# Conformer and S5 layer on one core: gate-row copies behind the first convolution taps, B loaded a step ahead, small matrices ahead of a tile's taps, two layer norm steps moved, last output tile halved

## Chip, core, metric

One Trainium2 chip, one of its cores, one launch. The metric is the device time of the whole kernel in microseconds (us). Data are float32; a product of two matrices is made of three TensorE passes over split operands (`hi*whi`, `lo*whi`, `hi*wlo`).

## The reference, cut to what matters

A layer with two branches beside each other over 2048 tokens of 1024 channels, with 256 tokens of context ahead of them:

```python
h = rmsnorm(x, norm_g) * (1 + scale) + shift                 # scale, shift, gate = silu(c) @ w_ada + b_ada
p = split(h @ w_in)                                          # 5 x 1024 columns: value, glu gate, conv gate, u, ssm gate
v = p[0] * sigmoid(p[1])
v = dwconv(v, 31 taps along rows or columns of a 64-wide grid) + conv_db
conv_out = silu(layernorm(v)) * silu(p[2])
y = s5(p[3]; a, b, c, both directions, state carried in from the context) + ssm_d * p[3]
y = gelu(y);  ssm_out = y * sigmoid(y @ glu_w + glu_b) * silu(p[4])
x = x + gate * (concat(conv_out, ssm_out) @ w_out)
return rmsnorm(x, final_g)
```

`gate` is a row of 1024 numbers. The S5 layer has 64 groups of 16 channels; `B` and `C` are complex matrices of a group.

## The kernel before

The kernel is one program of stages. By the trace's time: up to about 180 us the modulation and the first projections; from there to about 699 the other projections of `h`, with the convolution beside them; to about 1230 the state-space blocks; to about 1417 the GLU matrix product; to about 1791 the output product; then the end of the last output tile. The engines run their own queues in order, and a wait at the head of a queue holds everything behind it.

**Projections beside the convolution.** A projection (`project`, 24 matmuls of 512 columns, three for each of 8 slices, L129, L134 and L135) writes a bank `ps` from a pool of three. A convolution tile of 128 channels takes eight projections: four glu gates, which ScalarE evacuates (L296), and four values, which VectorE multiplies with them (`glu`, L299). So a projection can begin only when the bank of the projection three before it has been read. The 31 taps of the tile before are done on VectorE (L336, one instruction a tap and accumulator: `fP`, `fQ`, `fR`); the accumulators are begun by ScalarE (L319, L320, L323). After each projection `beside()` emits RATE = 4.8 taps, the glu products that are held, and one step of `toeplitz()`. That generator makes, for each of 16 channel groups, small matrices that the state-space stage needs, in four steps: (0) products on GpSimd; (1) every fourth group `bbar`, six VectorE products with `bq`, the loaded B, and a scratch tile `tb` (L363 to L368); (2) four VectorE additions into `ff` (L396); (3) 32 small matmuls into the bank `tz` (L407); their evacuation (`tzs`, L417 to L420) is at the head of the next group's step 0. TensorE's rows are chained in the order of the program, so a matmul of `tz` that waits holds the projections behind it.

**The gate rows.** Ahead of the first convolution tile, `gps` (one PSUM bank) collects the product of `silu(c)` with the gate columns of `w_ada` in four rows. ScalarE copies each row to a tile `gr` (L717) and SyncE stores it to `gate_d` (L718). `gr`, `tb`, `us`, and other short-lived tiles rotate through a pool `stage` with one tag, `"sa"`, of three buffers: a new tile waits until what stood in its buffer three tiles before has been used.

**Layer norm of the convolution.** It runs in four pieces of 512 tokens (`layer_norm(nb)`): load and sum (`lsum`, GpSimd), `mu` (L1069, matmul), `va` (L1082) and the reciprocal root with `dg` (L171), `rb` (L1101) with the products by it on VectorE and the silu on ScalarE, then four loads, products by the conv gate `lg` and stores to `mix_d`. The pieces are woven into TensorE's order at chosen products: piece 0 in the GLU stage by the list `aside` (`for n in (6, 10, 14, 15, 17, 18, 20, 21)`: one step after GLU product `n`), pieces 1 to 3 in the output stage by `LN_QUARTER = (0, 4, 7, 9)`.

**The output stage.** 16 tiles `t_` of 128 tokens, each with four products of 24 matmuls (half `k8` of the channels, half `i` of the columns) into `pso`. The product number within four tiles is `4 * (t_ % 4) + 2 * (1 - k8) + i`; counted over all tiles it is called product 0 to 63 here. A product needs its half of `mix_d` loaded (`mr`) and split into `mh` (ScalarE, L1026) and `ml` (VectorE, L1029), and the split rows of `w_out` (`woh`, `wol`). Tiles 4 to 7 use piece 1 of the layer norm, so product 18 (the convolution half of tile 4) is the first that needs it. The last tile ends with a square sum, a reciprocal root (`rs`), two products by `rs` and `fg` of 512 columns (L1287) and their stores (L1288).

Of the kernel before, what the change touches and what calls it, by code (L numbers as in the profile page):

```python
# [7 lines left out]
F32 = mybir.dt.float32  # L8
# [6 lines left out]
P = 128  # L15
# [10 lines left out]
GH = 16  # L26
# [6 lines left out]
LN_QUARTER = (0, 4, 7, 9)  # L33
# [44 lines left out]
def build(ctx: ExitStack, tc: tile.TileContext, ins: dict, out: bass.AP):  # L78
    nc = tc.nc
# [64 lines left out]
    for nb in (0, 1, 3):  # L144
        hpool[nb] = hstack.enter_context(tc.tile_pool(name=f"h{nb}", bufs=1, side="right"))
    nps = pstack.enter_context(tc.tile_pool(name="nps", bufs=2, space=PS))
# [154 lines left out]
    def taps(ct, v, half):  # L301
# [21 lines left out]
        act(r_, S_, AF.Identity, scale=tap[2](0), bias=db[:, 1, ct:ct + 1])  # L323
# [27 lines left out]
    def bbar(q):  # L351

        g_ = slice(16 * q, 16 * q + 16)
        shp = [P, 16, GH]
        bq = stage.tile([P, 2, 16, GH], F32, tag="sa", name="bq")
        for i, nm in enumerate(("b_re", "b_im")):
            nc.sync.dma_start(bq[:, i], ins[nm][:, g_, :])
        bb = late.fir.tile([P, 33, GH], F32, tag="bb", name="bb")
        tb = stage.tile(shp, F32, tag="sa", name="tb")
        bbr, bbn = bb[:, 0:16], bb[:, 16:32]  # L360
        nc.gpsimd.memset(bb[:, 32], 0.0)
        a, b = (t_[:, g_].unsqueeze(2).to_broadcast(shp) for t_ in (br, bi))
        dv(vt(bbr, bq[:, 0], a, op=MUL))  # L363
        dv(vt(tb, bq[:, 1], b, op=MUL))
        dv(vt(bbr, bbr, tb, op=SUB))
        dv(vt(bbn, bq[:, 0], b, op=MUL))
        dv(vt(tb, bq[:, 1], a, op=MUL))
        dv(st(bbn, bbn, -1.0, tb, op0=MUL, op1=SUB))  # L368
        return bb

    def toeplitz():

        for b4 in range(GR // 4):
            g0 = 4 * b4
            cc = late.fir.tile([P, 2, 4, GH], F32, tag="cc", bufs=2, name="cc")
            for i, nm in enumerate(("c_re", "c_im")):
                nc.sync.dma_start(cc[:, i], ins[nm][:, g0:g0 + 4, :])
            fs, sums = [], []
# [13 lines left out]
            if b4 % 4 == 0:  # L392
                bb = bbar(b4 // 4)
# [6 lines left out]
            tz = late.tps.tile([P, 2, P], F32, tag="tz", name="tz")  # L400
# [305 lines left out]
    gps = nps.tile([P, 512], F32, tag="gps", bufs=1, name="gps")  # L706
# [7 lines left out]
    for i in range(2):  # L714
        for c in range(2):
            gr = stage.tile([1, 512], F32, tag="sa", name="gr")
            act(gr, gps[64 * i + 32 * c:64 * i + 32 * c + 1], AF.Copy)  # L717
            nc.sync.dma_start(gate_d[i:i + 1, c * 512:(c + 1) * 512], gr)  # L718
# [4 lines left out]
    with tstack, tc.tile_pool(name="fir", bufs=1, reuse_waits="tile") as late.fir, \  # L723
            tc.tile_pool(name="firps", bufs=1, space=PS, reuse_waits="tile") as late.fps, \
            tc.tile_pool(name="tps", bufs=1, space=PS, reuse_waits="tile") as late.tps:
# [7 lines left out]
        def beside():  # L733

            due[0] += RATE
# [10 lines left out]
            next(toe, None)  # L746
# [37 lines left out]
        drain()  # L784
    vstack.close()
# [411 lines left out]
    for n in (6, 10, 14, 15, 17, 18, 20, 21):  # L1197
        aside[n].append(ln)
# [65 lines left out]
    with tc.tile_pool(name="op", bufs=2, reuse_waits="tile") as op:  # L1264
# [14 lines left out]
        def finish(t_, cols, xt, sq):  # L1279
# [6 lines left out]
            for cs_ in [slice(0, 1024)] if t_ < 15 else [slice(0, 512), slice(512, 1024)]:  # L1286
                st(xt[:, cs_], xt[:, cs_], rs, fg[:, cs_], op0=MUL, op1=MUL)  # L1287
                nc.sync.dma_start(ov[row(t_)[0], row(t_)[1], cs_], xt[:, cs_])  # L1288
# [3 lines left out]
        for t_ in range(16):  # L1292
# [16 lines left out]
            for k8 in (1, 0):  # L1309
# [6 lines left out]
                if t_ < 15:  # L1316
                    for i in range(2):
                        product(k8, i)
                        if k8 == 0:
                            evacuate(i, cols[i], pss[i], xt, sq)  # L1320
                        if t_ < 12 and 4 * (t_ % 4) + 2 * (1 - k8) + i in LN_QUARTER:
                            next(lns[t_ // 4 + 1])
            if t_ == 15:
                for i in range(3):
                    product(1, i)
                    product(0, i)
                    evacuate(i, cols[i], pss[i], xt, sq)
            finish(t_, cols, xt, sq)
# [75 lines left out]
```

## Time and profile before

| | |
|---|---|
| time, three runs | 1800.38, 1800.89, 1803.52 us; median 1800.89 |
| profiled execution | 1801.97 us, its span 1800.2 us |
| TensorE busy | 1725.8 us, 96% of the span |
| VectorE busy | 1410.8 us, 78% |
| ScalarE, GpSimd busy | 584.9 us (32%), 561.5 us (31%) |
| DMA engines | 39% on average |

The span is what the trace covers; the profiled execution's own time is 1.8 us longer. The share of an engine is an average over stages of very different kinds: TensorE is the busiest in all of them, but what it waits for, and which engine it is that sets its pace, must be read in each stage. A wait of TensorE costs more than its idle time, since the matmuls behind it are slower for a while.

### The profile page before, as it was taken

Reading aid. Unit: us, or ns where it says so; the run is one execution under the profiler, and the core shown is the slowest. Engines: PE = TensorE matmul, PEld = TensorE weight load, DVE = VectorE, ACT = ScalarE, POOL = GpSimd, SP = SyncE. Lnnn points to the kernel's source line nnn. Section 1 sums busy time; section 2 is a strip of 40 time slices with the busy share of each in tenths; the row PEclk is TensorE's granted clock in tenths of the full one; section 3 lists DMA queues with packets and bytes.
Section 4 is the critical chain, followed back from the end, with each engine's and each line's share of the span. In section 5 each row is a group of like instructions: output and inputs, shape, how many; then the busy total and the mean of one; then the engine's idle time right before and its main releaser. Section 6 shows DMA issues by size and latency. Waiting matters only on the chain.

```text
span 1800.2 us, 23670 instructions
## 1 busy us (share of the span) xinstructions
PE 1725.8 (96%) x8728; PEld 1354.6 (75%) x8728; DVE 1410.8 (78%) x2063; ACT 584.9 (32%) x904; POOL 561.5 (31%) x550
## 2 busy tenths in 40 slices
PE   7999799999999998999999999999989989999998
PEld 2675577787788886777777777778778768887887
DVE  7863799999998987999999999995665755656533
ACT  4542211221222113343433433354453422222211
POOL 0632243344432113665554655320210041212000
PEclk9999899999999998999999999999999999999999
DMA  9604131222222123243333333363738837363621
GB/s 342 231 18 127 34 104 44 96 79 68 97 98 76 50 76 109 88 121 106 101 117 115 98 122 105 105 225 120 215 113 279 303 108 206 118 198 122 176 97 44
DMA packets 175724, 227.45 MB, mean 126 GB/s; under 512 B 38516, under 2 KB 117492, under 8 KB 174584
## 3 DMA queue, kind: packets, MB, share of 16 engines
q1 hardware_dynamic: 175608, 225.94, 39.0%
q8 instruction: 69, 1.13, 0.3%
q14 instruction: 47, 0.39, 0.1%
HBM read 147.36 MB, written 78.52 MB: 125 GB/s over the span
## 4 chain that ended last, share of the span: by engine, by line
PE 65%; DVE 20%; DMA 6%; issue 3%; ACT 2%; POOL 2%; SPq 1%; DVEq 0%; ACTq 0%; POOLq 0%
PE ps L129 13%; PE ps L134 13%; PE ps L135 13%; PE pso L135 4%; PE pso L134 4%; PE pso L129 4%; DVE fQ L336 4%; PE S L894 3%; DVE fR L336 3%; PE Y L945 3%; DVE fP L336 3%; DMA mix_d<-lx 2%; PE Y L936 1%; DVE lo L223 1%; PE adps L620 1%
## 5 line engine op out<-in xcount | busy, mean ns | idle before, releaser
L129 PE MATMUL ps<-hi,whi 128*128 128x512 f32 x1248 | 499.1, 400 | 1.2 <-ACT v L296 1.2
L134 PE MATMUL ps<-lo,whi 128*128 128x512 f32 x1248 | 492.7, 395 | 0.0
L135 PE MATMUL ps<-hi,wlo 128*128 128x512 f32 x1248 | 491.6, 394 | 0.3 <-POOL wlo L244 0.3
L129 PEld LDWEIGHTS ps<-hi,whi 128*128 128x128 f32 x1248 | 235.9, 189 | 62.1 <-issue 9.3
L135 PEld LDWEIGHTS ps<-hi,wlo 128*128 128x128 f32 x1248 | 236.1, 189 | 55.5 <-issue 3.5
L134 PEld LDWEIGHTS ps<-lo,whi 128*128 128x128 f32 x1248 | 236.2, 189 | 53.4 <-issue 5.2
L129 PE MATMUL pso<-woh,mh 128*128 128x512 f32 (+1 forms) x528 | 206.2, 391 | 0.8 <-ACT woh L1026 0.4
L134 PE MATMUL pso<-wol,mh 128*128 128x512 f32 (+1 forms) x528 | 203.8, 386 | 2.1 <-DVE wol L1029 2.1
L135 PE MATMUL pso<-woh,ml 128*128 128x512 f32 (+1 forms) x528 | 204.4, 387 | 0.7 <-DVE ml L1029 0.5
L244 POOL TENSOR_TENSOR wlo<-wraw,whi 128x1024 fp32r<-128x1024 f32 x37 | 97.3, 2630 | 174.2 <-ACT whi L243 174.2
L336 DVE SCALAR_TENSOR_TENSOR fQ<-v,sml,fQ 128x960 f32<-128x960 f32 (+11 forms) x120 | 149.2, 1243 | 0.0
L336 DVE SCALAR_TENSOR_TENSOR fP<-v,sml,fP 128x960 f32<-128x960 f32 (+10 forms) x112 | 121.0, 1080 | 24.7 <-ACT fP L319 24.7
L336 DVE SCALAR_TENSOR_TENSOR fR<-fS,comb,fR 128x960 f32<-128x960 f32 (+11 forms) x120 | 128.1, 1067 | 0.0
L918 DVE TENSOR_TENSOR_SCAN t<-mag,t 128x287 f32<-128x287 f32 x128 | 122.0, 1011 | 0.0
L134 PEld LDWEIGHTS pso<-wol,mh 128*128 128x128 f32 x528 | 99.8, 189 | 24.7 <-DVE wol L1029 3.1
L129 PEld LDWEIGHTS pso<-woh,mh 128*128 128x128 f32 x528 | 99.8, 189 | 22.9 <-ACT woh L1026 1.4
L135 PEld LDWEIGHTS pso<-woh,ml 128*128 128x128 f32 x528 | 99.7, 189 | 21.7 <-DVE ml L1029 1.5
L243 ACT ACTIVATE whi<-wraw 128x1024 fp32r<-128x1024 f32 x37 | 39.1, 1055 | 212.2 <-PE ps L134 172.9
L129 PE MATMUL ps<-yh,gwh 128*128 128x512 f32 x256 | 100.7, 393 | 0.0
L134 PE MATMUL ps<-yl,gwh 128*128 128x512 f32 x256 | 99.9, 390 | 0.0
L135 PE MATMUL ps<-yh,gwl 128*128 128x512 f32 x256 | 99.9, 390 | 0.0
L1064 POOL TENSOR_TENSOR lsum<-lx 128x512 f32<-128x512 f32 x4 | 5.5, 1362 | 301.7 <-DMA lx<-cv_d 301.7
(295 smaller groups left out, 2804.8 us busy)
## 6 DMA issues: line engine op xcount, KB each, us to landing
wraw<-in_w_in SPq DMA_DIRECT2D x37, 512.0 KB
mr<-mix_d SPq DMA_DIRECT2D x32, 512.0 KB
wa<-in_w_ada SPq DMA_DIRECT2D x32, 256.0 KB
xt<-in_x_t SPq DMA_DIRECT2D x32, 256.0 KB
u_d<-us SPq DMA_DIRECT2D x32, 256.0 KB
f_d<-ff SPq DMA_DIRECT2D x32, 256.0 KB
cv_d<-v SPq DMA_DIRECT2D x8, 1024.0 KB
cg_d<-gs SPq DMA_DIRECT2D x32, 256.0 KB
```

Of the source, the lines that this page charges most:

```text
L129: i = nc.tensor.matmul(ps, wh, rh, start=first, stop=False)
L134: nc.tensor.matmul(ps, wh, rl, start=False, stop=False)
L135: last[0] = nc.tensor.matmul(ps, wl, rh, start=False, stop=end)
L223: st(lo, xts[k], sh_, hi.bitcast(F32), op0=ADD, op1=SUB)
L243: act(hi, raw, AF.Copy)
L244: pt(lo, raw, hi.bitcast(F32), op=SUB)
L336: yield st(at(acc, lo_ + o, hi_ + o), at(src, lo_ + j, hi_ + j), tap[n](j), at(acc, lo_ + o, hi_ + o), op0=MUL, op1=ADD)
L620: nc.tensor.matmul(adps[32 * c:32 * c + 32], sil[:, k], was[h, k, c], start=(k == 0), stop=(k == KT - 1), skip_group_check=True)
L894: m = nc.tensor.matmul(Sf[h_, o + c0:o + c1], k.E[:, d, i, h_], seq[g][d][:, c0:c1], start=True, stop=True, skip_group_check=True)
L918: nc.vector.tensor_tensor_scan(dst[:, d, 0:L], mag8[:, g0 + d:g0 + d + 1].to_broadcast([P, L]), src[:, d, 0:L], 0.0, op0=MUL, op1=ADD)
L936: m = nc.tensor.matmul(Y[:, g], k.M[:, g], k.U[:, g, NX:NCOL], start=True, stop=False, skip_group_check=True)
L945: m = nc.tensor.matmul(Y[:, g], k.F[h_, i, d], hs, start=False, stop=(i == 1 and d == 1), skip_group_check=True)
```

## The change

Five things are changed.

- The four copies of the gate rows and their stores move from ahead of the first tile's taps into the first `beside()`, behind the accumulators' begin on ScalarE (a dependency without a semaphore keeps them behind `late.fr`). `gps` and `tz` share a PSUM bank of a pool of their own, `gpp`; before, `gps` stood in the pool that was closed ahead of the convolution, and `tz` in one of its own.
- `bq` is loaded in step 0, by `b_load`, into a tile of its own in the pool `fir`; before, it was loaded in `bbar`, a step later, into the pool `stage`.
- `beside()` begins with `next(toe, None)`, ahead of its taps and glu products; before, it ended with it.
- Layer norm piece 0 has its `rb` step after GLU product 16 in place of 15, its first gate step at 18 and its second at 19. Piece 1 has its `mu`, `va` and `rb` steps one output product later: (0, 5, 8, 10).
- In the last tile each piece `xt` is multiplied by `fg` as it is evacuated (into `gx`); after `rs`, ScalarE scales columns 0 to 511 and VectorE columns 512 to 1023, and the two halves are stored from ScalarE's and SyncE's queues.

```diff
-LN_QUARTER = (0, 4, 7, 9)
+LN_QUARTER = ((), (0, 5, 8, 10), (0, 4, 7, 9), (0, 4, 7, 9))
...
+    gpp = tstack2.enter_context(tc.tile_pool(name="gpp", bufs=1, space=PS))
...
+    def b_load(q):
+        bq = late.fir.tile([P, 2, 16, GH], F32, tag="bq", name="bq")
+        for i, nm in enumerate(("b_re", "b_im")):
+            nc.sync.dma_start(bq[:, i], ins[nm][:, 16 * q:16 * q + 16, :])
+        return bq
+
+    def bbar(q, bq):
...
-        bq = stage.tile([P, 2, 16, GH], F32, tag="sa", name="bq")
-        for i, nm in enumerate(("b_re", "b_im")):
-            nc.sync.dma_start(bq[:, i], ins[nm][:, g_, :])
...
+            if b4 % 4 == 0:
+                bq = b_load(b4 // 4)
...
-            tz = late.tps.tile([P, 2, P], F32, tag="tz", name="tz")
+            tz = gpp.tile([P, 512], F32, tag="g", name="tz")[:, 0:2 * P].rearrange("p (d q) -> p d q", d=2)
...
+    def gate_out():
+        for i in range(2):
+            for c in range(2):
+                gr = stage.tile([1, 512], F32, tag="sa", name="gr")
+                g_ = act(gr, gps[64 * i + 32 * c:64 * i + 32 * c + 1], AF.Copy)
+
+                tc.add_manual_dep(g_.ins, late.fr.ins.name, mybir.DependencyInfo(
+                    mybir.DependencyClass.NoSync, mybir.DependencyReason.DATA), reason="order")
+                nc.sync.dma_start(gate_d[i:i + 1, c * 512:(c + 1) * 512], gr)
...
         def beside():
 
+            next(toe, None)
             due[0] += RATE
...
-            next(toe, None)
+            if late.fr is not None and not late.gated:
+                late.gated = True
+                gate_out()
...
-    for n in (6, 10, 14, 15, 17, 18, 20, 21):
+    for n in (6, 10, 14, 16, 18, 19, 20, 21):
...
-            for cs_ in [slice(0, 1024)] if t_ < 15 else [slice(0, 512), slice(512, 1024)]:
-                st(xt[:, cs_], xt[:, cs_], rs, fg[:, cs_], op0=MUL, op1=MUL)
-                nc.sync.dma_start(ov[row(t_)[0], row(t_)[1], cs_], xt[:, cs_])
+            if t_ < 15:
+                st(xt, xt, rs, fg, op0=MUL, op1=MUL)
+                nc.sync.dma_start(ov[row(t_)[0], row(t_)[1], :], xt)
+                return
+
+            act(xt[:, 0:512], late.gx[:, 0:512], AF.Identity, scale=rs)
+            vs(xt[:, 512:1024], late.gx[:, 512:1024], rs, None, op0=MUL)
+            nc.scalar.dma_start(ov[row(t_)[0], row(t_)[1], 0:512], xt[:, 0:512])
+            nc.sync.dma_start(ov[row(t_)[0], row(t_)[1], 512:1024], xt[:, 512:1024])
...
+                    if i == 0:
+                        late.gx = wp.tile([P, 1024], F32, tag="wraw", bufs=1, name="gx")
+                    vt(late.gx[:, cols[i]], xt[:, cols[i]], fg[:, cols[i]], op=MUL)
```

Line numbers of the changed kernel are 2 higher at the taps and the glu (L338, L301), 5 at `bbar` (L368 to L373), 7 at `ff`, `tz` and `tzs` (L403, L414, L426), 9 at the gate rows (L726) and 17 in the layer norm (L1086, L1118).

On ScalarE, at the end of the first convolution tile, the rows of before are these (`whi` and `us` belong to projections, `v` is a glu gate):

```order
L320 ACTIVATE fQ<-v,sml 128x32x32
L243 ACTIVATE whi<-wraw 128x1024
L428 ACTIVATE us<-ps 128x2x256
L296 ACTIVATE v<-ps 128x512 x2
L717 ACTIVATE gr<-gps 1x512 x4
L319 ACTIVATE fP<-v,db,sml 128x1024
L323 ACTIVATE fR<-fS,db,comb 128x1024
```

And these are the rows of the changed kernel at the same place:

```order
L321 ACTIVATE fP<-v,db,sml 128x1024
L322 ACTIVATE fQ<-v,sml 128x32x32
L325 ACTIVATE fR<-fS,db,comb 128x1024
L245 ACTIVATE whi<-wraw 128x1024
L435 ACTIVATE us<-ps 128x2x256
L298 ACTIVATE v<-ps 128x512 x2
L726 ACTIVATE gr<-gps 1x512 x4
```

`fP` and `fR` now stand beside `fQ`, ahead of two gates of the next tile and of the four copies `gr`.

On VectorE the rows behind the sum `fS`, the last thing before the first tap, were these before, with what each waits for (`DMAHW` is a transfer):

```order
L336 SCALAR_TENSOR_TENSOR fP_1752<-v_1326,sml_159,fP_1752 128x32x31 [waits Activation_49]
...
L336 SCALAR_TENSOR_TENSOR fQ_1753<-v_1326,sml_159,fQ_1753 128x32x30 [waits DVE_49]
L363 TENSOR_TENSOR bb_1814<-bq_1811,br_480 128x256 [waits DMAHW5_49]
L364 TENSOR_TENSOR tb_1815<-bq_1811,bi_481 128x256 [waits DMAHW3_49,DMAHW4_49,DMAHW1_49,DMAHW7_49,DMAHW0_49,PE_49]
...
L368 SCALAR_TENSOR_TENSOR bb_1814<-bb_1814,tb_1815 128x256 [waits DVE_49]
...
L396 TENSOR_TENSOR ff_1766<-ff_1766,pp_1767 128x256 [waits Pool_49]
```

Eight taps stood ahead of `bbar` and five between it and the `ff` additions. The changed kernel has:

```order
L338 SCALAR_TENSOR_TENSOR fP_1760<-v_1329,sml_159,fP_1760 128x32x31 [waits Activation_49]
L338 SCALAR_TENSOR_TENSOR fQ_1761<-v_1329,sml_159,fQ_1761 128x32x31 [waits Activation_49]
L338 SCALAR_TENSOR_TENSOR fR_1762<-fS_1759,comb_987,fR_1762 128x32x31 [waits Activation_49]
L368 TENSOR_TENSOR bb_1809<-bq_1742,br_483 128x256 [waits DMAHW7_49]
L369 TENSOR_TENSOR tb_1810<-bq_1742,bi_484 128x256 [waits DMAHW1_49,DMAHW2_49,DMAHW0_49,DMAHW5_49,PE_49,Activation_49]
...
L373 SCALAR_TENSOR_TENSOR bb_1809<-bb_1809,tb_1810 128x256 [waits DVE_49]
...
L403 TENSOR_TENSOR ff_1745<-ff_1745,pp_1746 128x256 [waits Pool_49]
```

Three taps now stand ahead of `bbar` and five between it and `ff`; `tb` takes the buffer of the second `gr` copy, and waits for ScalarE (that copy) and for its store too.

On TensorE the rows around `mu` of piece 1 were these before (`pso_12057` and `pso_12058` are the two halves of tile 1's columns):

```order
L135 MATMUL pso_12057<-woh_11762,ml_12063 128x512
L1069 MATMUL mu_12092<-lsum_11951,cst_157 128x512
L129 MATMUL pso_12058<-woh_11575,mh_12062 128x512
L134 MATMUL pso_12058<-wol_11576,mh_12062 128x512
L135 MATMUL pso_12058<-woh_11575,ml_12063 128x512
```

In the changed kernel they are:

```order
L135 MATMUL pso_12058<-woh_11762,ml_12063 128x512
L1086 MATMUL mu_12116<-lsum_11951,cst_157 128x512
L129 MATMUL pso_12057<-woh_11802,mh_12149 128x512
L134 MATMUL pso_12057<-wol_11803,mh_12149 128x512
L135 MATMUL pso_12057<-woh_11802,ml_12150 128x512
```

`mu` stands 24 matmuls, one product, later; `va` and `rb` of piece 1 and `rb` of piece 0 move in the same way, and nothing else on TensorE changes place.

## Rows read from the trace of the kernel before

**Rows 1.** Table by stretch: time, PE, PEld, DVE, ACT, POOL busy; clock; DMA share; GB/s.
```profile
240.00:700.00 460.00, 450.23 (x2307) 363.00 (x2305) 438.42 (x480) 97.08 (x129) 142.69 (x139) 0.99 0.23 82
...
1340.00:1430.00 90.00, 90.00 (x398) 74.47 (x397) 55.67 (x71) 38.29 (x42) 0.00 (x0) 1.00 0.84 270
...
sum 1800.20, PE 1725.82 PEld 1354.58 DVE 1410.84 ACT 584.87 POOL 561.48; mean PE 172.58 PEld 135.46 DVE 141.08 ACT 58.49 POOL 56.15
```

**Rows 2.** Waits of PE over the span: us in total, times, longest.
```profile
PE tz L407 <- DVE ff L396: 21.6, 10, 12.7
...
PE mu L1069 <- POOL lsum L1066: 6.4, 2, 5.6
PE rb L1101 <- DVE dg L171: 5.4, 1, 5.4
...
PE pso L134 <- DVE wol L1029: 2.1, 3, 0.8
```

**Rows 3.** Waits of DVE from 191 to 696 us.
```profile
DVE fP L336 <- ACT fP L319: 24.7, 1, 24.7
DVE v L299 <- PE ps L135: 11.8, 4, 4.3
```

**Rows 4.** Timeline of ACT, 162 to 192 us: start, duration, instruction, idle before and releaser.
```profile
187.46 2.44 ACT L717 ACTIVATE gr<-gps 1x512 f32<-1x512 f32 x4 [1.28 <-PE gps L701]
189.80 1.19 ACT L319 ACTIVATE fP<-v,db,sml 128x1024 f32<-128x1024 f32 x1
```

**Rows 5.** Timeline of DVE, 160 to 213 us.
```profile
165.14 1.23 DVE L322 TENSOR_TENSOR fS<-v 128x1024 f32<-128x1024 f32 x1
191.02 1.26 DVE L336 SCALAR_TENSOR_TENSOR fP<-v,sml,fP 128x992 f32<-128x992 f32 x1 [24.65 <-ACT fP L319]
...
201.81 0.41 DVE L364 TENSOR_TENSOR tb<-bq,bi 128x256 f32<-128x256 f32 x1
...
209.36 1.42 DVE L396 TENSOR_TENSOR ff<-ff,pp 128x256 f32<-128x256 f32 x4
```

**Rows 6.** Timeline of SP's queue, 186 to 192 us.
```profile
188.07 1.44 SPq L718 DMA_DIRECT2D gate_d<-gr  x3
```

**Rows 7.** Timeline of PE at 194 to 216 and at 455 to 466 us.
```profile
209.92 2.50 PE L407 MATMUL tz<-ff,bb 64*32 64x128 f32 x32 [12.73 <-DVE ff L396]
...
458.60 0.41 PE L407 MATMUL tz<-ff,bb 64*32 64x128 f32 x4 [2.61 <-DVE ff L396]
...
465.76 0.39 PE L134 MATMUL ps<-lo,whi 128*128 128x512 f32 x1
```

**Rows 8.** Timeline of DVE and PE at 440 to 446 us, the fifth convolution tile.
```profile
442.40 1.16 DVE L299 TENSOR_TENSOR v<-ps,v 128x512 f32<-128x512 f32 x1
...
444.84 0.39 PE L129 MATMUL ps<-hi,whi 128*128 128x512 f32 x1
445.07 0.39 PE L134 MATMUL ps<-lo,whi 128*128 128x512 f32 x1
```

**Rows 9.** Timeline of PE, 1318 to 1332 us.
```profile
1327.67 2.08 PE L1101 MATMUL rb<-dg,cst 128*128 128x128 f32 x8 [5.39 <-DVE dg L171]
```

**Rows 10.** Timeline of PE, 1444 to 1462 us.
```profile
1454.41 2.07 PE L1069 MATMUL mu<-lsum,cst 128*128 128x512 f32 x2 [5.58 <-POOL lsum L1066]
1455.50 1.42 PE L129 MATMUL pso<-woh,mh 128*128 128x512 f32 x1
...
1460.12 0.60 PE L129 MATMUL pso<-woh,mh 128*128 128x512 f32 x1
```

**Rows 11.** Timelines of PE and DVE, 1484 to 1534 us.
```profile
1486.66 1.05 PE L1101 MATMUL rb<-dg,cst 128*128 128x128 f32 x8
...
1530.99 1.23 DVE L1029 TENSOR_TENSOR ml<-mr,mh 128x1024 fp32r<-128x1024 f32 x1 [8.85 <-ACT mh L1026]
```

**Rows 12.** Timelines of DVE and SP's queue at the end.
```profile
1795.58 1.42 DVE L1287 SCALAR_TENSOR_TENSOR ox<-ox,orsy,fg 128x512 f32<-128x512 f32 x2
1796.36 0.99 SPq L1288 DMA_DIRECT2D out<-ox  x2
```

## What the change was predicted to do

> **What bounds the kernel now.** I began with the table by stretch [rows 1]: TensorE is busy for 1725.8 of 1800.2 us, so some 74 us are idle, and the change can only work on them, on the slower matmuls behind them, and on the end. The waits of TensorE by releaser [rows 2] say where: 21.6 us in ten waits of `tz` for VectorE's `ff`, one of 12.7; 5.6 us of `mu` for the sum `lsum`; 5.4 us of `rb` for `dg`; 2.1 us of the output products for `wol`.
>
> In the stage of projections the share misleads. From 240 to 700 us TensorE is busy for 450 of 460 us, but VectorE for 438 [rows 1], and from 191 us on it waits only for TensorE, four times, 11.8 us in all, after one wait of 24.7 us for `fP` [rows 3]. Up to those waits VectorE's queue is full, and TensorE is ahead of it only by what the three banks `ps` allow. VectorE sets the pace there, though TensorE's share is higher: what the change gives TensorE counts only as far as VectorE comes forward too. The tightest place that I found is in the fifth tile: the glu product that frees a bank ends at 443.56 (442.40 and 1.16) and the projection that needs it begins at 444.84 [rows 8], 1.3 us later.
>
> **The front: the gate rows' copies and the earlier steps.** Before, ScalarE's four copies of `gr` wait for the last matmul of `gps`, run from 187.46 for 2.44 us, and only then comes `fP` at 189.80 [rows 4]; VectorE, done with `fS` at 166.4, has its first tap at 191.02 [rows 5]. In the changed order `fP`, `fQ`, `fR` come behind the glu gate of the first tile, so the first taps begin between 166.4 (`fS` done) and 168.8 (two of ScalarE's instructions, 1.19 each [rows 4], later). That would be 22 to 25 us, but the wait is not gone. After three taps and one product of `bbar` stands `tb`, which takes the second `gr`'s buffer: it waits for that copy and for its store. A copy takes 0.61 us (2.44 by four), so the second ends at 187.46 + 1.22 = 188.68 and its store is issued then. How long a store takes to free its buffer has no row of its own. The fourth copy takes the first one's buffer and starts without a gap at 189.3, while the first store was issued at 188.07 [rows 4, 6], so it is 1.2 us at most. At zero VectorE goes on at 188.7, at 1.2 at 189.9; I take 189.9, as the bound is the only row.
>
> The Trainium skill (DMA: Bandwidth & Descriptors, Anatomy of one DMA) gives, for transfers that GpSimd issues, a fixed cost of about 2 us each, most of it the receipt of the write. The trace's bound of 1.2 us does not agree; by the page VectorE would go on at 190.7 and the sum below would be 0.8 us less.
>
> From 189.9: five products of `bbar` at 0.41 (2.0), five taps at 1.26 (6.3) and `ff` (1.4) [rows 5] end at 199.6. TensorE stood at 209.92 - 12.73 = 197.2 [rows 7], so its first wait of 12.7 becomes one of 2.4 us, 10.3 less. VectorE itself comes forward less. Before, its first tap began at 191.02; now it has three taps (3.8) and one product (0.4) behind it when it goes on at 189.9: 191.0 - 189.9 + 4.2, or 5.3; with taps overlapping a little I take 5.0.
>
> The moved `next(toe)` puts the four `ff` additions ahead of four or five taps, some 5 us earlier on VectorE relative to its own queue, and 1.4 us of work ahead of the glu products that then stand behind it. It works on the other `tz` waits, 21.6 - 12.7 = 8.9 us idle. One of them as a sample, at 458.60: TensorE idle from 455.99, the last of the 16 further matmuls at 465.76 [rows 7], 9.8 us for what takes 1.0 + 16 x 0.23 = 4.7 unbroken (0.23 from the two rows of [rows 8]): 5.1 lost, 2.2 of it slow matmuls. Up to the fifth tile TensorE can be at most 1.3 us nearer to VectorE than before [rows 8], so at 445 us it is at most 5.0 + 1.3 = 6.3 us earlier, whatever happens to `tz`: the rest of the 10.3 comes back as waits for a glu product. Behind that tile the 5.1 us wait of `tz` goes: 11.4. I take 10, since each glu product now stands behind an `ff` and some of the new waits will be felt there; the ends are 6 (nothing passes behind 445) and 13 (glu products come 1.5 us sooner than I think). Late next is the glu product.
>
> Loading B earlier costs nothing: two issues on SP's queue come a step sooner, behind the loads of C, and their data are needed a step later; uncovered it would be a wait of VectorE for a transfer, 1.2 us by the store's bound, four times. The bank shared by `gps` and `tz` adds a wait of `tz` for copies that end at 189.9, with `tz` due at 199.
>
> **Piece 0 of the layer norm.** `rb` waited 5.39 us, until 1327.67 [rows 9]; one GLU product (24 x 0.23 = 5.5) later it finds `dg` ready. With slow matmuls of about 1.8, as behind the wait of the sample, TensorE is up to 7.2 us earlier afterwards. But the next thing it waits for is `wol`, 2.1 us at the start of the output stage [rows 2], the end of a chain of loads in a stretch where the DMA engines are 84% busy [rows 1]. The chain begins with piece 0's gate steps: the third and fourth stay at GLU products 20 and 21, so come 7.2 us sooner, the first and second are one product later, so 1.7 sooner. Between 1.7 and 7.2 I take 4.5.
>
> **Piece 1.** `mu` waited 5.58 us, and the nine steps from 1455.50 to 1460.12 took 4.62 in place of 2.07 [rows 10]: 8.1 us. One product later the sum is there but for 0.1 us: 8.0 gained. `rb` is also one product later, and it is the head of a chain: `rb` at 1486.66, products on VectorE, silu, gate loads, stores to `mix_d`, load, `ml` at 1530.99 [rows 11], 44.3 us. Eight products lie between it and product 18, 1.05 + 8 x 5.49 = 45.0, so the chain is just in time. With seven it is 5.5 us late: a new wait of `pso` for `ml`, with slow matmuls of 2.2 again, 7.7 lost. Net 0.3 gained. Ends: 4 gained (a chain that shortens because its loads meet less traffic), 1.5 lost.
>
> **The tail.** Two products of 512 columns take 1.42 us [rows 12], one behind the other; on two engines the second store is issued up to 0.7 sooner. The product with `fg` moves behind each evacuation, beside ScalarE's square sum; uncovered it would cost 0.7. Both halves then share the DMA engines. I take 0.6, from 0 to 0.7. Of the issues the Trainium skill (Trainium Kernel Development and Optimization, Key Constraints) says that queues of several engines run on the same 16 DMA engines, and issuing from several saves only issue time. By the issues' row, 0.99 us for two, that would be a gain of 0.3, and the sum 0.3 us less.
>
> **Sum.** 10.0 + 4.5 + 0.3 + 0.6 = 15.4 us. The profiled execution took 1801.97 us, 1.1 above the median; its span should go from 1800.2 to 1784.8, and the median from 1800.9 to 1785.5.
>
> **Rivals.**
> - *The front pays in full.* If `tb` found its buffer free, VectorE would run from 167 us, all `tz` waits would go, and the front would give 21.6: 1800.9 - 27.0 = 1773.9. Against it stands the order, where `tb` waits for ScalarE and a transfer.
> - *Piece 1's chain is not in the way.* If the chain behind `rb` shrinks with what is ahead of it, the 8.0 us stay: 1777.8. For it: the chain goes through transfers, which share the DMA engines with other loads; against it: its length was that of the eight products to 0.7 us, and nothing in the change shortens it.
> - *The loads set the start of the output stage.* At 84% the chain to `wol` may not move at all; then piece 0 gives nothing: 1790.0.
> - *Slower.* TensorE now runs up to 1.3 us nearer to VectorE's 28 glu products (four in each of seven tiles) than it did, and each time it falls idle its next matmuls cost 2.2 us more. Up to seven such falls (15.4 by 2.2) only eat the gain; nine make it slower by 0.2%; with twelve the time is 1785.5 + 26.4 = 1811.9. For it: 1.3 us is all the room there is. Against it: VectorE sets the pace there, and TensorE then loses what it would have waited for anyway.
> - *Nothing.* If VectorE's wait for the gate store reaches 195 us, its shift is zero, and with the loads holding piece 0 too only 1 to 3 us are left: 1799.
>
> **Chances.** Forecast 0.45, free `tb` 0.10, piece 1 kept 0.17, loads 0.20, slower 0.05, nothing 0.03. The first four cases hold 0.92. The range, 1774 to 1793, leaves out the two last and about half of the free `tb`, and takes in the front's lower end (1789.5) and the loads' case with 3 us less of the front. The forecast's own range is 1780 to 1790. A measurement of this kernel tells about 0.2%, 3.6 us, from no change. Faster by more: 0.92; within: 0.03; slower: 0.05.
>
> **What would show it.** VectorE's first taps at 167, then a wait of some 18 us of `tb` with a transfer or ScalarE as releaser, ending near 190; the first wait of `tz` at 2 to 3 us and the others gone or small, with new waits of `ps` (L129) for `glu` in their place; no wait of `rb` at 1322; `mu` without its 5.6; a new wait of `pso` for `ml` of 5 to 6 us at product 18; the two last stores issued together. The forecast is wrong if `tb` does not wait, if the projections keep their distance from the glu products, if `wol` comes no sooner, or if product 18 does not wait.

## The result, and the profile after

The changed kernel took 1779.59 us, the median of four runs (1775.71 to 1781.56), where the kernel before took 1801.59 (1800.38 to 1803.52) beside it: a ratio of 0.9874 (95% interval 0.9854 to 0.9894), 22 us less. Run again on another chip it took 1778.11 beside 1803.95, 0.9846 (0.9819 to 0.9874). The forecast was 1785.5, its own range 1780 to 1790, the whole range 1774 to 1793. The direction and the whole range hold; the first median lies 0.4 us below the forecast's own range, and the gain is 22 to 26 us where 15.4 were worked out. The rival in which the 8.0 us of piece 1 stay, 1777.8, came nearer than the forecast.

The profiled execution, 1775.71 us, has a span of 1773.9, 26.3 less than before. Its waits of TensorE (us in total, times, longest) answer to [rows 2]:

```profile
PE ps L129 <- DVE v L301: 12.1, 6, 3.8
...
PE pso L134 <- DVE wol L1046: 2.6, 4, 0.8
...
PE tz L414 <- DVE ff L403: 1.5, 2, 1.3
...
PE rb L1118 <- DVE dg L173: 0.9, 1, 0.9
```

`tz` has gone from 21.6 us to 1.5, and `ps` waits for the glu product (L301) 12.1 us, a row that was not there. `mu` has no row any more (ten other traces with a later `mu` show 0.4 to 1.7 us), `rb` has 0.9 of 5.4, `wol` is about as it was (2.1).

VectorE around the gate rows, the timeline that answers to [rows 5]:

```profile
166.14 1.26 DVE L338 SCALAR_TENSOR_TENSOR fP<-v,sml,fP 128x992 f32<-128x992 f32 x1
...
168.47 1.25 DVE L338 SCALAR_TENSOR_TENSOR fR<-fS,comb,fR 128x992 f32<-128x992 f32 x1
169.63 2.40 DVE L368 TENSOR_TENSOR bb<-bq,br 128x256 f32<-128x256 f32 x1
189.99 0.42 DVE L369 TENSOR_TENSOR tb<-bq,bi 128x256 f32<-128x256 f32 x1 [17.97 <-ACT gr L726]
...
197.69 1.42 DVE L403 TENSOR_TENSOR ff<-ff,pp 128x256 f32<-128x256 f32 x4
```

The wait of 24.65 us ahead of the first tap is gone, and 17.97 of it stand three taps later, at `tb`. ScalarE's copies and their stores on SP's queue run as before:

```profile
187.16 2.43 ACT L726 ACTIVATE gr<-gps 1x512 f32<-1x512 f32 x4 [1.24 <-PE gps L708]
```
```profile
187.78 2.06 SPq L730 DMA_DIRECT2D gate_d<-gr  x4
```

The second copy ended at 188.4 (187.16 and half of 2.43), its store was issued then, and `tb` went on 1.6 us later. The row names ScalarE, but the copy it needs had been done for 1.6 us: what came last was the store. The bound worked out from before was 1.2; in toe_back, below, `tb` goes on 1.25 us behind the same issue (189.56 less 188.31; its copies begin at 187.09), so the store itself needs no more than that. The Trainium skill (DMA: Bandwidth & Descriptors, Anatomy of one DMA) has about 2 us for transfers that GpSimd issues; these runs, in which SyncE issues, stay below it.

On TensorE the first wait of `tz`, 12.73 us in [rows 7], is 1.31, and the waits for a glu product are at other places:

```profile
198.26 0.41 PE L414 MATMUL tz<-ff,bb 64*32 64x128 f32 x4 [1.31 <-DVE ff L403]
...
293.72 0.79 PE L129 MATMUL ps<-hi,whi 128*128 128x512 f32 x1 [3.75 <-DVE v L301]
...
488.65 0.80 PE L129 MATMUL ps<-hi,whi 128*128 128x512 f32 x1 [3.01 <-DVE v L301]
...
1317.47 1.16 PE L1118 MATMUL rb<-dg,cst 128*128 128x128 f32 x8 [0.89 <-DVE dg L173]
...
1438.08 1.02 PE L1086 MATMUL mu<-lsum,cst 128*128 128x512 f32 x2
...
1467.32 1.05 PE L1118 MATMUL rb<-dg,cst 128*128 128x128 f32 x8
```

The chain from `rb` of piece 1 to product 18, on SP's queue and on VectorE, answers to [rows 11]:

```profile
1500.40 0.80 SPq L1040 DMA_DIRECT2D mr<-mix_d  x2
```
```profile
1479.22 0.69 DVE L1046 TENSOR_TENSOR lx<-lx,lg 128x512 f32<-128x512 f32 x1 [0.90 <-DMA lg<-cg_d]
...
1506.03 1.23 DVE L1046 TENSOR_TENSOR ml<-mr,mh 128x1024 fp32r<-128x1024 f32 x1 [3.41 <-ACT mh L1043]
```

It took 38.7 us (1506.03 less 1467.32) where it took 44.3 before. The end, which answers to [rows 12]:

```profile
1769.57 0.49 DVE L1309 TENSOR_SCALAR ox<-gx,orsy 128x512 f32<-128x512 f32 x1
1769.62 0.72 ACT L1308 ACTIVATE ox<-gx,orsy 128x512 f32<-128x512 f32 x1 [2.58 <-issue]
1770.09 0.34 SPq L1311 DMA_DIRECT2D out<-ox  x1
1770.37 0.38 ACTq L1310 DMA_DIRECT2D out<-ox  x1
```

Both halves run beside each other; from the first product by `rs` to the end it is 4.3 us (1773.9 less 1769.57), before 4.6 (1800.2 less 1795.58).

**Where the time went, by stage.** Each length below is the distance between two rows of TensorE's timeline in the profiled execution: *front* from the end of the projection ahead of the first `tz` to the end of the last projection (the `et` row's start less its idle time); *GLU* from the first matmul of the GLU product to product 0; then products 0 to 2, 3 to 5 and 6 to 17; *end* from the last matmul's end to the end of the span. Between the front and the GLU product all kernels took 532.7 to 534.7 us, from product 18 to the last matmul's end 260.0 before and 258.5 to 260.8 in the others. Of before there is one trace.

| kernel | front | GLU | 0 to 2 | 3 to 5 | 6 to 17 | end |
|---|---|---|---|---|---|---|
| before | 501.9 | 185.1 | 20.4 | 26.1 | 67.7 | 8.7 |
| changed | 491.9 | 178.1 | 21.5 | 16.9 | 68.1 | 8.4 |
| after_again | 488.5 | 178.8 | 22.2 | 18.2 | 68.1 | 8.4 |
| tb_free | 483.9 | 178.2 | 23.6 | 18.3 | 68.1 | 8.4 |
| toe_back | 494.4 | 178.2 | 23.0 | 17.3 | 68.1 | 8.4 |
| bank_back | 493.1 | 178.2 | 22.6 | 17.4 | 68.4 | 8.4 |
| ln1_back | 488.3 | 178.2 | 22.4 | 24.1 | 67.7 | 8.4 |
| rb9 | 491.5 | 178.5 | 22.0 | 18.8 | 68.1 | 8.4 |
| rb11 | 491.9 | 178.5 | 23.7 | 18.0 | 75.6 | 8.4 |
| tail_back | 489.6 | 178.7 | 21.6 | 16.9 | 68.2 | 8.7 |
| ln_back | 492.0 | 184.6 | 20.8 | 23.8 | 67.7 | 8.4 |
| rb0_back | 488.3 | 185.6 | 20.2 | 17.7 | 68.3 | 8.4 |
| best_a | 483.9 | 178.1 | 23.1 | 18.6 | 68.1 | 8.4 |
| best_b | 480.3 | 178.5 | 23.5 | 18.5 | 68.2 | 8.4 |

Eight of the kernels have the changed front, as their edits lie behind it, and it took 488.3 to 492.0 us in them: 3.7 us of chance, which a time contains too. So an edit of a later stage is read from its own columns.

### The profile page after: what moved, and what is told of

It reads as the page before. It is cut to its first block, busy times and chain, and to the rows that moved or that the text cites. A ratio compares the mean times of both kernels' runs of the same rounds, so it can differ in the third digit from the quotient of the medians.

```text
span 1773.9 us, 23678 instructions
## 1 busy us (share of the span) xinstructions
PE 1717.9 (97%) x8728; PEld 1350.3 (76%) x8728; DVE 1413.1 (80%) x2065; ACT 585.8 (33%) x905; POOL 561.0 (32%) x550
## 3 DMA queue, kind: packets, MB, share of 16 engines
q1 hardware_dynamic: 175464, 225.68, 39.5%
## 5 line engine op out<-in xcount | busy, mean ns | idle before, releaser
L129 PE MATMUL ps<-hi,whi 128*128 128x512 f32 x1248 | 499.1, 400 | 13.3 <-DVE v L301 12.1
L338 DVE SCALAR_TENSOR_TENSOR fQ<-v,sml,fQ 128x960 f32<-128x960 f32 (+11 forms) x120 | 147.4, 1228 | 0.0
L338 DVE SCALAR_TENSOR_TENSOR fR<-fS,comb,fR 128x960 f32<-128x960 f32 (+11 forms) x120 | 127.9, 1066 | 0.0
L338 DVE SCALAR_TENSOR_TENSOR fP<-v,sml,fP 128x960 f32<-128x960 f32 (+10 forms) x112 | 120.9, 1080 | 0.1
L134 PEld LDWEIGHTS pso<-wol,mh 128*128 128x128 f32 x528 | 99.2, 188 | 24.7 <-DVE wol L1046 4.1
```

The lines of the kernel that those rows point to most:

```text
L129: i = nc.tensor.matmul(ps, wh, rh, start=first, stop=False)
L134: nc.tensor.matmul(ps, wh, rl, start=False, stop=False)
L338: yield st(at(acc, lo_ + o, hi_ + o), at(src, lo_ + j, hi_ + j), tap[n](j), at(acc, lo_ + o, hi_ + o), op0=MUL, op1=ADD)
```

## Experiments

Three sets of four, each on one chip, with the kernel before beside them (medians 1803.95, 1803.28 and 1804.57 us). All edits are of the changed kernel.

### after_again: the changed kernel once more

No edit. 

> The changed kernel once more, beside the experiments on one chip. Expected is 1776 to 1782 us, 20 to 25 less than before. In the trace the front should be 10 us shorter at the end of the projections, as in the first profile; the place that may differ from run to run is the wait for ml at product 18, from nothing to 4 us.

1778.11 us. The front is 13.4 us shorter than before, and product 18 waits 0.3 us:

```profile
1505.90 0.50 PE L135 MATMUL pso<-woh,ml 128*128 128x512 f32 x1 [0.29 <-DVE ml L1046]
```

### tb_free: no wait for the gate store

```diff
-        tb = stage.tile(shp, F32, tag="sa", name="tb")
+        tb = late.fir.tile(shp, F32, tag="tb", name="tb")
```

> The changed kernel, with a buffer of its own for tb in place of the one of the second gate-row copy. Theory 1 (the wait of tb for that copy and its store holds VectorE back and so sets the front): VectorE goes on at 170 us, ff is done near 181, no tz wait and no wait for a glu product is left; between 197 and 689 us the changed kernel loses some 22 us against unbroken matmuls, and most of it goes: 12 to 22 us less than the changed kernel, 1758 to 1768. Rival (the three banks ps and the glu products limit TensorE however early VectorE begins, or VectorE then waits for TensorE's tz): 0 to 4 us less, 1775 to 1780.

1768.47 us, 9.6 less than the changed kernel beside it: between the two theories, and most of it (4.6 to 8) in the front. `tz` finds `ff` done, some 16 us before it is needed:

```profile
179.72 1.42 DVE L403 TENSOR_TENSOR ff<-ff,pp 128x256 f32<-128x256 f32 x4
...
199.21 0.17 DVE L426 TENSOR_TENSOR tzs<-tzs,tz 128x16 f32<-128x16 f32 x1 [6.92 <-ACT tzs L425]
```

But then VectorE waits for TensorE (its next `tzs` needs what ScalarE takes out of the bank of `tz`), which reaches `tz` at 197, as every kernel does at 196 to 198, and waits of TensorE for a glu product are still there:

```profile
196.96 1.08 PE L414 MATMUL tz<-ff,bb 64*32 64x128 f32 x32
```
```profile
PE ps L129 <- DVE v L301: 8.1, 4, 3.0
```

So the store did hold the front back, and it was not the only limit: 8.1 of the 12.1 us of waits for a glu product are left.

### toe_back: the steps behind the taps again

```diff
         def beside():
-            next(toe, None)
...
+            next(toe, None)
```

> The changed kernel with the step of toeplitz at the end of beside again, behind the taps. Theory 1 (VectorE's shift sets the front): eight taps, not three, now stand ahead of tb, so VectorE comes forward 10.8 us (1.1 and 9.7 of taps and one product) in place of 5; the first tz wait is about 2, the later tz waits come back as they were before; the front gains about 10.8 against before, and the time is within 2 us of the changed kernel, 1778 to 1782. Rival (it was the reordered steps that took the tz waits away): the tz waits come back and cost 9 to 10 us, 1787 to 1790.

1781.52 us, 3.4 more than the changed kernel; the front is 2.4 to 6 us longer, and 7.5 shorter than before. The waits of TensorE and of VectorE:

```profile
PE tz L414 <- DVE ff L403: 13.6, 16, 2.6
```
```profile
DVE tb L369 <- ACT gr L726: 13.1, 1, 13.1
```

The `tz` waits are back. But `tb` waits 13.1 us and not 18.0, as eight taps now stand ahead of it. Two thirds of the front's gain come without the reordered steps: theory 1 is nearer, though it had hoped for all of it.

### bank_back: the gate rows' copies ahead of the taps again

```diff
...
-    gps = gpp.tile([P, 512], F32, tag="g", name="gps")
+    gps = nps.tile([P, 512], F32, tag="gps", bufs=1, name="gps")
...
-            tz = gpp.tile([P, 512], F32, tag="g", name="tz")[:, 0:2 * P].rearrange("p (d q) -> p d q", d=2)
+            tz = late.tps.tile([P, 2, P], F32, tag="tz", name="tz")
...
+    gate_out()
     xstack.close()
...
-        late.fr, late.gated = None, False
+        late.fr, late.gated = None, True
...
```

> The changed kernel with gps in the old pool and tz in a bank of its own, so that the accumulators' begin waits for the gate-row copies again, as before; the reordered steps and the rest stay. Theory 1: VectorE begins at 191 us, ff is done near 204, the first tz wait is some 7 us; up to 445 us TensorE can only be 1.3 us nearer to VectorE, behind it the 5 us of one tz wait go: 6.4 gained at the front against before in place of 10.2, so 3 to 5 us slower than the changed kernel, about 1783. Rival (all of the front came from the gate rows): 10 us slower, about 1790.

1782.20 us, 4.1 more than the changed kernel, as theory 1 has it; the front is 493.1, 8.8 shorter than before where 6.4 were expected. The waits of VectorE and of TensorE:

```profile
DVE fP L336 <- ACT fP L319: 24.6, 1, 24.6
```
```profile
PE tz L412 <- DVE ff L401: 5.9, 1, 5.9
```

Either half of the front's change alone gives 7.5 to 9 us, both together 10 to 13.6. They work on the same waits. The earlier load of B stands in both, and no run took it back; before, VectorE did not wait for it either [rows 3].

### ln1_back: piece 1 where it was

```diff
-LN_QUARTER = ((), (0, 5, 8, 10), (0, 4, 7, 9), (0, 4, 7, 9))
+LN_QUARTER = ((), (0, 4, 7, 9), (0, 4, 7, 9), (0, 4, 7, 9))
```

> The changed kernel with piece 1 of the layer norm at (0, 4, 7, 9) again. Prediction's term (the chain from rb to ml has a fixed length of 44 us, so one product later gives back what mu gains): within 2 us of the changed kernel, 1776 to 1781. Theory 2 (the chain's length is not fixed: with rb one product later it was 37 us, so nothing was given back): mu waits 5.5 us again with slow matmuls behind it, product 18 waits at most 1 us in both, and the time is 8 us longer, 1784 to 1788.

1778.57 us, within 0.5 of the changed kernel on another chip, and 3.5 more than rb9 on its own. By the time alone the prediction's term would stand. The trace says otherwise:

```profile
1433.78 1.72 PE L1086 MATMUL mu<-lsum,cst 128*128 128x512 f32 x2 [4.85 <-POOL lsum L1083]
```

`mu` waits again, products 3 to 5 take 24.1 us in place of 16.9 to 18.8, and products 6 to 17 only 0.4 less: 5 to 7 us lost. The profiled execution has one of the two shortest fronts (488.3); the changed kernel's own medians, 1779.6 and 1778.1, differ by 1.5. Medians over four runs whose fronts differ by chance don't settle 5 us; ln_back against rb0_back, below, is the other pair that differs in this edit alone.

### rb9 and rb11: rb of piece 1 one product sooner, one later

```diff
-LN_QUARTER = ((), (0, 5, 8, 10), (0, 4, 7, 9), (0, 4, 7, 9))
+LN_QUARTER = ((), (0, 5, 8, 9), (0, 4, 7, 9), (0, 4, 7, 9))
```

(rb11 has 11 in place of 9.)

> The changed kernel with rb of piece 1 at product 9 in place of 10, mu at 5 and va at 8 as changed: (0, 5, 8, 9). Theory 2a (the chain's length goes by where rb stands in the rhythm of the mixed tiles' loads and splits, which TensorE's products pace): the chain is 42 us long again, a load of a mixed tile is issued 6 us behind rb and the next splits come 11 and 22 us behind it; product 18 waits as little as now, and the time is that of the changed kernel within 2 us. Theory 2b (the chain is 37 us whenever the traffic of the start of the stage is out of the way): it stays at 37 us, product 18 has 5 us to spare; the time is 0 to 2 us less.

> The changed kernel with rb of piece 1 one product later still, at 11: (0, 5, 8, 11). Six products, 33 us, lie between it and product 18. If the chain is 37 us and 1 us of split, product 18 waits about 5 us, with slow matmuls behind it 5 to 8 us more than the changed kernel, 1782 to 1786. If the chain were 44 us, as the prediction had it, the wait would be 11 and the time 1790.

rb9 took 1775.07 us (1771.67 to 1778.61), 3 to 4.5 less than the changed kernel on other chips, which neither theory expected and best_a, below, does not bear out; it has no wait at product 18. rb11 took 1787.05 and has one of 7.3, more than was expected:

```profile
1518.68 0.80 PE L129 MATMUL pso<-woh,mh 128*128 128x512 f32 x1 [7.27 <-ACT mh L1043]
```

The length of the chain, from the end of `rb` to the start of `mh` for product 18, in every trace: with `rb` at 9 it is 42.2 (before), 39.5 (ln_back), 39.7 (ln1_back), 40.7 (rb9), 38.5 and 40.8 (the last two kernels); with `rb` at 10 it is 36.3 to 37.5 in seven traces, the first of the changed kernel among them at 36.6; with `rb` at 11 it is 39.1, with TensorE itself waiting in it. So the length goes with the place of `rb`, as theory 2a has it, and the trace of before had the longest sample of these. But the place is not all. The trace of before has the chain three times, each begun at product 9: 42.2 us for piece 1, 43.2 for piece 2, and 33.3 for piece 3, whose products by `rb` and whose `mh` are

```profile
1670.80 4.87 DVE L1029 TENSOR_TENSOR lx<-lx,rb 128x512 f32<-128x512 f32 x8 [5.67 <-PE rb L1101]
```
```profile
1704.02 1.06 ACT L1026 ACTIVATE mh<-mr 128x1024 fp32r<-128x1024 f32 x1 [3.52 <-DMA mr<-mix_d]
```

In all traces piece 2 has 40.3 to 43.2 us and piece 3 has 33.1 to 33.8. Eight loads `lx` of the next piece stand on SP's queue among those of the chain in pieces 1 and 2, none in piece 3; that they make the difference is not shown. In rb9 a load of 512 KB for a mixed tile is issued 6.1 us behind `rb` and the second product waits 3.2 us for its gate:

```profile
1472.01 0.32 SPq L1040 DMA_DIRECT2D mr<-mix_d  x1
```
```profile
1477.73 0.69 DVE L1046 TENSOR_TENSOR lx<-lx,lg 128x512 f32<-128x512 f32 x1 [3.22 <-DMA lg<-cg_d]
```

With `rb` at 10 that load is issued 4 us ahead of the end of `rb` (1464.13 in the first trace), and the second product waits 0.9. That this load is the cause is argued from these rows; no run took it away by itself.

### tail_back: the last tile's end as before

```diff
-            if t_ < 15:
-                st(xt, xt, rs, fg, op0=MUL, op1=MUL)
-                nc.sync.dma_start(ov[row(t_)[0], row(t_)[1], :], xt)
-                return
-
-            act(xt[:, 0:512], late.gx[:, 0:512], AF.Identity, scale=rs)
-            vs(xt[:, 512:1024], late.gx[:, 512:1024], rs, None, op0=MUL)
-            nc.scalar.dma_start(ov[row(t_)[0], row(t_)[1], 0:512], xt[:, 0:512])
-            nc.sync.dma_start(ov[row(t_)[0], row(t_)[1], 512:1024], xt[:, 512:1024])
+            for cs_ in [slice(0, 1024)] if t_ < 15 else [slice(0, 512), slice(512, 1024)]:
+                st(xt[:, cs_], xt[:, cs_], rs, fg[:, cs_], op0=MUL, op1=MUL)
+                nc.sync.dma_start(ov[row(t_)[0], row(t_)[1], cs_], xt[:, cs_])
...
-                    if i == 0:
-                        late.gx = wp.tile([P, 1024], F32, tag="wraw", bufs=1, name="gx")
-                    vt(late.gx[:, cols[i]], xt[:, cols[i]], fg[:, cols[i]], op=MUL)
```

> The changed kernel with the last tile's end as before: two products by rs and fg on VectorE, both stores from SyncE's queue. In the first trace of the changed kernel the stretch from the last matmul's start to the end is 8.67 us, before it was 8.96; here 8.9 to 9.0 is expected, so 0.3 us more, less than a time can tell. The last 96 matmuls of 256 columns took 11.2 us with the change, 10.8 before: if the products with fg on VectorE slow them, they take 10.8 here; if it is something else, 11.2.

A single run: 1776.86 us, and the end is 8.7 us long, as before, where the changed kernels have 8.4. The last matmuls of 256 columns still take 11.2 us, so the products with `fg` are not what slowed them; ln1_back, with the changed tail, has the 10.8 of before. Why they differ stays open; it is 0.4 us.

### ln_back and rb0_back: both pieces where they were, piece 0 where it was

```diff
-    for n in (6, 10, 14, 16, 18, 19, 20, 21):
+    for n in (6, 10, 14, 15, 17, 18, 20, 21):
```

(ln_back has the edit of ln1_back too.)

> The changed kernel with both pieces of the layer norm where they were before: (6, 10, 14, 15, 17, 18, 20, 21) and (0, 4, 7, 9). What is left is the front and the tail. If the traces of the changed kernel are read rightly, the front gives 10 us and the tail nothing, so 1790 to 1793, and the two layer norm moves together give 12 to 15 us. By the prediction's terms for them (4.5 and 0.3) the moves give 5 us and this kernel takes 1782 to 1785. In the trace rb of piece 0 should wait 5 us and mu of piece 1 5 us.

> The changed kernel with piece 0 of the layer norm where it was before, piece 1 as changed. By the traces piece 0's move gives 6 to 7 us at the start of the output stage and 1 of them is lost again to wol: 1784 to 1786. By the prediction's term 4.5 us: 1782 to 1784. By its rival (the loads set the start of the output stage) nothing: 1778 to 1780.

ln_back took 1789.03 us, a ratio of 0.9914 (0.9899 to 0.9929): the front and the tail alone give 15.5 us of time, more than the 10 to 14 of the stages, with the kernel before at 1804.57 in this set and 1801.97 in its trace. That is nearer to the 1790 to 1793 of the traces than to the prediction's 1782 to 1785. rb0_back took 1782.86 (1778.42 to 1786.53), 6.2 less on the same chip: that is piece 1's move. It lies where the prediction's 4.5 us for piece 0 put it, and 3 to 5 us above the changed kernel; by the stages, at the end of this section, the rival in which the loads hold the output stage's start and the move gives nothing is out. In both, `rb` of piece 0 waits again; of ln_back and of rb0_back:

```profile
PE rb L1118 <- DVE dg L173: 5.3, 1, 5.3
```
```profile
PE rb L1118 <- DVE dg L173: 5.8, 1, 5.8
```

Together the two moves give 9 to 11 us (1789.0 less 1779.6 and 1778.1, on different chips), less than the 12 to 15 expected and twice the 4.8 of the prediction. The GLU stage and products 0 to 2 take 205.4 and 205.8 us together here, 205.5 before, and 199.6 to 202.2 in the eleven kernels with piece 0 moved, 201.0 on average: 4.5 us.

### best_a and best_b: what the runs point to

best_a is tb_free with `rb` of piece 1 at 9. best_b has, besides, the held glu products first:

```diff
         def beside():
+            while held:
+                dv(glu(*held.pop()))
             next(toe, None)
```

> The changed kernel with tb in a buffer of its own and rb of piece 1 at product 9 (0, 5, 8, 9). The two gains lie in different stages, so they should add: 9 to 10 us for tb, 0 to 3 for rb: 1765 to 1769.

> The same, and in beside() the held glu products come first, ahead of the step of toeplitz and the taps. With tb free the four waits of TensorE for a glu product, 8 us, and up to 5 us of slow matmuls behind them are left at the front. Theory 1 (they wait because bbar, ff and taps stand ahead of the glu product in VectorE's queue): they go, and the time is 6 to 12 us less than without: 1755 to 1762. Rival (VectorE's work as a whole sets the pace): the waits go to tz or to the next tile, and the time is the same within 3 us.

best_a took 1769.26 us, best_b 1767.69, ratios of 0.9806 (0.9792 to 0.9821) and 0.9796 (0.9780 to 0.9813): both 9 to 12 us faster than the changed kernel, and not to be told apart from tb_free (0.9795); the 0 to 3 us of `rb` at 9 do not show. In best_b no wait for a glu product is left, so it was the place in VectorE's queue that made them, and short ones of `tz` have come back:

```profile
PE tz L414 <- DVE ff L403: 5.1, 11, 2.0
```

Its front is 3.6 us shorter than best_a's and its median 1.6, where 6 to 12 were hoped for. Fronts of one kind differ as much by chance, so a gain is not shown, and the rival, in which the waits go to `tz`, is nearer. Two waits for the state-space stage, `et` (6.4 us) and `S` (2.6), and those ahead of the projections are untouched by all of this.

## Why the prediction was right, and where it was short

**Which engine sets the pace at the front: right.** That the wait at `fP` moves to `tb` and ends at 189.9 (measured 189.99), that the first `tz` wait becomes 2.4 (1.3), that the others go and waits for glu products take their place (none before, 12.1 us after) all stand in the rows. The term of 10.0 us measured 9.9 to 13.6, 11.7 on average over the eight traces with this front. The rival in which `tb` doesn't wait was run as tb_free: the `tz` waits go, but with 8.1 us of waits for a glu product left it is worth 9.6 us of time more, not 11.6.

How the 10.0 was put together did not hold. The prediction allowed TensorE 6.3 us up to 445 us, "whatever happens to `tz`", because it read 1.3 us between a glu product and "the projection that needs it" [rows 8]. The same two in the first trace of the changed kernel:

```profile
433.10 1.15 DVE L301 TENSOR_TENSOR v<-ps,v 128x512 f32<-128x512 f32 x1
```
```profile
433.58 0.39 PE L129 MATMUL ps<-hi,whi 128*128 128x512 f32 x1
```

That projection now begins before the glu product ends at 434.25, so it does not need it; in the program the one behind it does, and that one began at 450.34 before, 6.8 us behind the glu product. So the 1.3 us were not the room. Counted from the start of the front, the projection comes 11.0 us sooner (11.9 in after_again, and 7.3 in bank_back, where 1.3 were expected). Later TensorE is 16 to 17 us ahead and gives back 6.1 us in the first trace and 3.5 in after_again, at the wait for a glu product near 490 us and the matmuls behind it; the prediction put 1.4 there. That a bound set too low and a give-back set too low meet at 10 is luck.

**Piece 0: right.** Forecast 4.5; the GLU stage and products 0 to 2 show 4.5 between the kernels with and without the move. As foreseen TensorE gets its `rb` gain, some 6.7 us, and gives 1 to 3 back at the start of the output stage. How much it gives back was not worked out: 4.5 was taken between 1.7 and 7.2, and that it is met so closely is luck.

**Piece 1: the step that failed.** The prediction said: "With seven it is 5.5 us late: a new wait of `pso` for `ml`". It took the 44.3 us from `rb` to `ml` as a fixed length, though the trace that it was read from has the same chain 9 us shorter in piece 3. The chain was 38.7 us after the change, so product 18 waits at most some tenths; by the prediction's own sign ("if product 18 does not wait") this part of it was wrong. Products 3 to 17 took 93.8 us before, 91.8 and 91.6 in the two kernels with piece 1 put back, and 85.1 to 86.9 in the ten others that have `rb` at 9 or 10 behind a later `mu`: 5 to 6 us by this edit, where the term was 0.3; by time, 6.2 between ln_back and rb0_back and 0.5 or less between ln1_back and the changed kernel. The rival that kept the 8.0 us was right in kind, but nothing in the prediction could tell why; the reason that it gave against itself, that nothing in the change shortens the chain, was wrong, since the place of `rb` does; that it does so by the mixed tiles' loads is argued, not shown. The give-back is real one product further on: in rb11 it costs 7.4 us up to product 18.

**The tail: half of it.** Forecast 0.6, measured 0.3. From the first product by `rs` to the end of the last issue it was 1.77 us (1797.35 less 1795.58) and is 1.18 (1770.75 less 1769.57), so the issues end 0.6 us sooner and the span gets half of that; where the other half goes is not shown. The Trainium skill's sentence (Trainium Kernel Development and Optimization, Key Constraints), that several queues save only issue time, was turned into 0.3 in the prediction, by a step that is not given; the trace agrees with the size.

**The sum.** The terms as the stages show them: 11.7, 4.5, 5 to 6 and 0.3, less 0.4 for the slower last matmuls, 21 to 22 us, against a measured 22.0 and 25.8. Some 2 us more lie in products 3 to 5: 26.1 in the trace of before, 24.1 and 23.8 in the two kernels with piece 1 put back; one trace of before can't say whether that is chance. The slower rival, more lost behind many glu waits, had six or seven such waits and not nine, and one of them cost nothing more in one run and 2.8 us in another; its ground, 1.3 us as all the room, was the misreading above.

## What to carry to other kernels

Ask of a wait that a change takes away what stands next in the same queue on the same buffers: here 18 of 24.7 us stood again at a scratch tile that shared its ring with the very copies moved out of the way, and a buffer of its own was worth 10 us. The chain through loads and stores had no fixed length: measure such a chain in several places (here three pieces in one trace: 42, 43 and 33 us) and ask what it shares the queues with, before it is used as the price of a shift. And when an edit is worth 5 us and the runs spread over 5, compare the length of its own stage in the traces.

## What the runs showed of the hardware

That the matmuls behind a wait of TensorE are slower for a while holds for some waits only. The same wait, in the same place of the same program, was followed by slow matmuls in one run and not in another. The windows around the wait of 3.01 us at 488.65 in the first trace of the changed kernel and around its twin of 3.02 us at 487.21 in after_again (columns as in [rows 1]: the granted clock is the third number from the end):

```profile
484.00:502.00 18.00, 14.99 (x81) 11.51 (x80) 17.93 (x27) 1.49 (x3) 6.97 (x7) 0.81 0.12 36
```
```profile
482.50:500.50 18.00, 14.98 (x93) 11.71 (x92) 17.93 (x27) 2.09 (x4) 8.46 (x9) 1.00 0.18 60
```

And the matmuls behind them, of the first trace and of after_again:

```profile
493.08 0.63 PE L134 MATMUL ps<-lo,whi 128*128 128x512 f32 x1
493.51 0.63 PE L135 MATMUL ps<-hi,wlo 128*128 128x512 f32 x1
```
```profile
488.01 0.39 PE L129 MATMUL ps<-hi,whi 128*128 128x512 f32 x1
488.24 0.39 PE L134 MATMUL ps<-lo,whi 128*128 128x512 f32 x1
```

Steps of 0.43 us on the one side, 0.23 on the other; the clock had fallen to its lower level, 1.2 GHz, for some thirteen matmuls in one run and not in the other. From the first matmul behind the wait to the next `tz` it is 8.5 us in the one (488.65 to 497.11) and 5.7 in the other (487.21 to 492.91), 2.8 of difference, most of the 3.4 us by which the two fronts differ. So the price of this wait is not a number but either of two, and the spread of the changed kernel's runs, 3 to 6 us, is of the size that two or three of its six or seven waits for a glu product can make; that they make all of it was not shown.
